# The first norm's modulation loaded and used by feature quarters, in a two-block transformer kernel on one core

## The chip, the cores and the metric

The kernel runs on one core of one Trainium2 chip. The metric is the device time of one execution in microseconds, the median of three runs. A core has five engines that each work through their own list of instructions in order: TensorE (PE, whose weight loads the profile lists apart as PEld), VectorE (DVE), ScalarE (ACT), GpSimd (POOL) and SyncE (SP), which issues the transfers here. An engine that stands before an instruction whose input is missing waits there, and what is behind it in its list waits too.

## The reference

Two blocks run one after the other on 256 tokens and 256 context tokens of width 1024. The first block has two layers; only the start of layer 0 is touched by the change:

```python
mod = silu(c) @ w_ada[li] + b_ada[li]               # 6 * 1024 values; the same for the context with c_ctx
sh1, sc1, g1, sh2, sc2, g2 = split(mod, 6)
m  = unpack(modulate(rms_norm(x,  norm1_w), sh1,  sc1)  @ w_in[li])
mc = unpack(modulate(rms_norm(xc, norm1_w), sh1c, sc1c) @ w_in[li])
...                                                  # attention, a gated recurrence, a Fourier mix
x = x + g1 * merge(...)
x = x + g2 * conv_ffn(modulate(rms_norm(x, norm2_w), sh2, sc2), ...)

def rms_norm(x, w):    return x * rsqrt(mean(x * x) + 1e-6) * w
def modulate(h, shift, scale): return h * (1 + scale) + shift
```

So before the first product with `w_in` can start, the kernel needs the token sums of squares, their roots, and the shift and scale of the features that the product reads. Shift and scale together are 2048 columns of `w_ada`, 8 MB of the 252 MB that the kernel reads.

## The kernel before

Activations lie with features on the 128 partitions: `x` is a tile of 8 feature steps (k) by 512 tokens (v = 0 the 256 tokens, v = 1 the context). Weights arrive as plain float32 tiles `raw`; ACT rounds them to `wH` (line 137) and DVE takes the rest `wL` (line 139). Each product of a feature step is three matmuls on TensorE, `wH` with the high part of the activation, `wH` with its low part, `wL` with the high part (line 151). The activation's parts are the tiles `hm`, a pair for each k.

The stages of the start, with the names that the text uses:

- **Squares.** `sq_add` squares `x` on ACT in pieces of 256 tokens and adds them up on DVE into `acc`; `rstd` lets TensorE add up over the partitions (line 204), ACT takes the root (line 210), DVE inverts and puts it on a diagonal (`dg`), TensorE spreads it over the partitions (line 222).
- **Modulation.** `ada_half` loads half of shift and half of scale, 16 tiles of 256 KB, and multiplies them with `csil`, the silu of the conditions, into one PSUM tile `pa` (line 315). `ada_out` copies that to `araw` on ACT, turns it on TensorE (line 373) and adds the bias on DVE into `mod`; `ada_scale` makes the factor `A`.
- **Norm and modulate.** `norm` multiplies `x` by the spread root on DVE (line 394). `modulate` then makes the high part `hm` on ACT (line 406), the full value `y` on POOL (line 408, two buffers) and the low part on DVE (line 409).
- **First products.** `rec(0)` makes four outputs, two forget gates from one weight (PSUM tiles `pg`) and query and gate from another (`ps`). They are 4 outputs x 8 feature steps x 3 = 96 products, each on 512 tokens. Both weights come in two parts of four feature steps, `wpart(*w, 0, 4)` and `(4, 8)`.
- After that `values()` follows, and beside it `ada_steps`, which loads the other columns of `w_ada` into `araw` tiles (line 332) and multiplies them (line 335). `ada_out` and `ada_steps` share the three buffers of `araw`.

`pa` has one buffer, so the product of the next piece of modulation waits until DVE has read the piece before:

```python
return self.ps.tile([P, 512], F32, name=tag, tag=tag, bufs=2 if tag in ("pg", "ps") else 1)
```

The order of the instructions on each engine is set when the program is built: a scheduler simulates the program and lists each engine's work by readiness and priority (`urgent` raises it). On the chip that order is fixed. All transfers here go through SP's list, in order.

Of the kernel before, what the change touches and what calls it, by code (L numbers as in the profile page):

```python
# [18 lines left out]
P = 128  # L19
EPS = 1e-6  # L20
KD = 8
# [34 lines left out]
class Builder:  # L56
# [104 lines left out]
    def gemm(self, W, c0, acts, T, t0=0, pt=None, tag=None):  # L161
# [10 lines left out]
        self.tick()  # L172
        return pt

    def gemm_nat(self, W, acts, t0, pt, p0):

        nc = self.nc
        H, L = W
        n, tot = 0, 3 * len(acts)
        for k, (h, l) in enumerate(acts):  # L180
            for c, a in ((h, H), (h, L), (l, H)):
                self.product(pt[:, p0:p0 + 256], c[:, t0:t0 + P], a[:, k, :], n == 0, n == tot - 1)
                n += 1
        self.tick()
# [46 lines left out]
    def setup(self, es):  # L231
# [21 lines left out]

        self.x = self.cp.tile([P, 8, 512], F32, name="x")
        self.mods = []

    def late_setup(self):
        nc, d = self.nc, self.d
# [4 lines left out]
        for a, b in ((0, 4), (4, 7)):  # L263
# [3 lines left out]
        self.sub = self.cp.tile([P, 2, P], F32, name="sub")  # L267
        nc.sync.dma_start(self.sub, bass.AP(tensor=d["subln"].tensor, offset=d["subln"].offset,
                                            ap=[[0, P], [P, 2], [1, P]]))

        v = self.vec("lam").rearrange("p (l a b) -> p l a b", l=2, a=2)
        pr = self.sml("lpr", [P, 4], bufs=1)
# [4 lines left out]
        nc.scalar.activation(ex, pl[:, 0:4], AF.Exp)  # L277
        self.nlam = self.cp.tile([P, 2], F32, name="nlam")
        for li in range(2):
            init = 0.8 - 0.6 * math.exp(-0.3 * li)  # L280
            nc.vector.tensor_scalar(self.nlam[:, li:li + 1], ex[:, 2 * li + 1:2 * li + 2], ex[:, 2 * li:2 * li + 1],
                                    init, op0=OP.subtract, op1=OP.subtract)
            nc.vector.tensor_scalar(self.sub[:, li], self.sub[:, li], 1.0 - init, None, op0=OP.mult)

        lb = self.vec("lb").rearrange("p (l c) -> p l c", l=2)
        w = self.sml("lbw", [P, 4, 4], bufs=1)
# [8 lines left out]
        nc.vector.tensor_scalar(self.lb1[:, 1], self.lb1[:, 0], -1.0, 1.0, op0=OP.mult, op1=OP.add)  # L295


    def ada_half(self, li, b, tags):

        nc, d = self.nc, self.d  # L300
        if b == 0:
            self.mods.append(self.cp.tile([P, 2, 48], F32, name=f"mod{li}"))
        pa = self.psum("pa")
        for k in range(KD):
            src = d["w_ada"][li, k * P:(k + 1) * P, 0:2048].rearrange("p (m h c) -> p h m c", m=2, h=2)[:, b]
            if tags[2 * k]:
                raws = [self.ring(tags[2 * k + m], [P, 512]) for m in range(2)]
                for m in range(2):
                    nc.sync.dma_start(raws[m], src[:, m])
            else:  # L310
                raw = self.wp.tile([P, 2, 512], F32, name="raw", tag="raw", bufs=3)
                nc.sync.dma_start(raw, src)
                raws = [raw[:, 0], raw[:, 1]]
            for g in range(4):
                nc.tensor.matmul(pa[32 * g:32 * g + 32, 0:256], self.csil[:, k, :],
                                 raws[g // 2][:, (g % 2) * 256:(g % 2) * 256 + 256],
                                 start=k == 0, stop=k == KD - 1)
        self.ada_out(li, pa, [(g // 2) * 8 + b * 4 + (g % 2) * 2 for g in range(4)], 2)

    def ada_steps(self, li, b):  # L320

# [231 lines left out]
        return oT  # L553


    def layer(self, li, states):
        nc, d = self.nc, self.d
        T = 512 if li == 0 else 256
# [1 line left out]
        h = [self.pair("hm", 512, F32R) for _ in range(KD)]  # L560
        if li == 0:
            self.rush = False
            tags = ["e"] * 4 + ["mo"] * 4 + ["uf"] * 2 + ["va"] * 2 + ["ka"] * 2 + ["qa"] * 2
            self.ada_half(0, 0, tags)
            first = [(self.wtiles(), d["w_in"][0, i]) for i in (8, 6)]
            for w in first:
                self.wpart(*w, 0, 4)
            tags = ["Kp"] * 3 + ["Qp"] * 3 + ["Sd", "So"] + ["vh"] * 2 + ["fg"] * 2 + ["kk"] * 2
            self.ada_half(0, 1, [None] * 2 + tags)
            for w in first:  # L570
                self.wpart(*w, 4, 8)
        pb = [None] * 2
        for v in (1, 0):
            with self.urgent():
                pb[v] = self.rstd(states[v])[:, 0:256]
        tags = ["on", "on", "aT", "ks", "qh", "sg", "tot"]
        n = [(k, v, self.norm(pb[v], v, k, tags[(k + 1 - v) % 7])) for k in range(0, KD, 2) for v in (1, 0)]
        mod = self.mods[li]
        A1 = self.cp.tile([P, 2, 8], F32, name=f"A1{li}")
        for k0 in (0, 4):  # L580
            self.ada_scale(li, 1, A1, k0, k0 + 4)
            for k, v, t in n[k0:k0 + 4]:
                self.modulate(t, v, k, A1, mod[:, :, 0:8], h)
        if li == 0:
            self.late_setup()
        acts = h
        W = lambda i: self.wload(d["w_in"][li, i])
        mo = [None] * 8
        va, qa, kT = {}, {}, {}
# [36 lines left out]
                nc.scalar.copy(vn[s].rearrange("p a c -> p (a c)"), pt)  # L626

        def rec(j, tag=None):
            w = first[0][0] if li == j == 0 else W(8 + 2 * j)
            fg = [self.ring("fg", [P, 2, 256]) for _ in range(2)]  # L630
            kk = [self.ring("kk", [P, 2, 256]) for _ in range(2)]
            for a in range(2):
                pt = self.gemm(w, a * P, acts, 512)
# [8 lines left out]
            w = first[1][0] if li == j == 0 else W(6 + j)  # L642
            pt = self.gemm(w, 0, acts, T, tag=tag)
            q = self.ring("qh", [P, T])
            nc.scalar.copy(q, pt)
            pt = self.gemm(w, P, acts, T, tag=tag)
# [628 lines left out]
    def build(self):  # L1275
        nc, tc = self.nc, self.tc
        with ExitStack() as es:
# [11 lines left out]
            st = [dict(), dict()]  # L1289
            for k in range(0, KD, 2):  # L1290
                nc.sync.dma_start(self.x[:, k:k + 2], self.d["xin"][:, k:k + 2])
            for k in range(KD):
                for v in (1, 0):
# [99 lines left out]
def layout(inp):  # L1393
# [5 lines left out]
    o["w_ada"] = g["w_ada"]  # L1399
    win = []  # L1400
    for li in range(2):
        w = g["w_in"][li].reshape(1024, 24, P)
# [57 lines left out]
```

## Time and profile before

| | |
|---|---|
| median of three runs | 1746.14 us (1745.81 to 1746.52) |
| the profiled execution | 1746.53 us, its span 1744.7 us |
| TensorE busy | 1694.4 us, 97% of the span |
| DVE, ACT, POOL busy | 1020.3, 844.6, 314.8 us |
| read from memory | 252.42 MB, 145 GB/s over the span |
| TensorE's mean granted clock | 0.99 |

The span is what the profiler saw; about 1.8 us lie around it. Times of rows are microseconds from the span's start.

### The profile page before, as it was taken

The page shows a single profiled execution, that of the slowest core. Times are in us where ns is not written, and L with a number is a line of the kernel's source. Part 1 is how long each engine was busy: PE and PEld are TensorE (multiplying, and loading weights), DVE is VectorE, ACT ScalarE, POOL GpSimd, SP SyncE. Part 2 cuts the span into 40 slices and gives each one's busy share as a digit, 9 for nine tenths or more (in the row PEclk, how much of TensorE's full clock was granted, in tenths as well). Part 3 has the DMA queues.
Part 4 walks back from the last instruction along what each step waited for, and adds up shares of the span by engine and source line. Part 5 has one row for each costly group of instructions (what it writes and reads, how often), then busy time and mean ns, then how long its engine had stood idle before and what let it go on. Part 6 is the DMA issues. An engine that isn't in the chain of part 4 may idle for free.

```text
span 1744.7 us, 29180 instructions
## 1 busy us (share of the span) xinstructions
PE 1694.4 (97%) x11598; PEld 1445.1 (83%) x11598; DVE 1020.3 (58%) x1835; ACT 844.6 (48%) x1472; POOL 314.8 (18%) x406
## 2 busy tenths in 40 slices
PE   6999899999999999989999899999999999999998
PEld 2766676887777788868788899999999999998988
DVE  4445756565433454455766776767666655655557
ACT  4435645453321343243755554665444565556554
POOL 1322210130100011234140210122202203212200
PEclk9999999999999999989999899999999999999999
DMA  9664111334445322335423446555555555444442
GB/s 331 231 199 151 46 44 36 98 119 147 161 140 187 130 97 72 103 112 176 147 91 105 153 149 207 176 176 190 178 189 180 178 175 173 156 146 148 155 135 71
DMA packets 86705, 255.45 MB, mean 146 GB/s; under 512 B 8823, under 2 KB 20471, under 8 KB 86568
## 3 DMA queue, kind: packets, MB, share of 16 engines
q1 hardware_dynamic: 86568, 253.58, 43.9%
q8 instruction: 91, 1.49, 0.3%
q14 instruction: 46, 0.38, 0.1%
HBM read 252.42 MB, written 1.13 MB: 145 GB/s over the span
## 4 chain that ended last, share of the span: by engine, by line
PE 92%; DVE 3%; ACT 2%; DMA 2%; issue 1%; POOL 0%; SPq 0%; ACTq 0%; DVEq 0%; POOLq 0%
PE pg L151 46%; PE ps L151 16%; PE ph L151 8%; PE pu L151 8%; PE pa L335 3%; PE ph L485 2%; PE ps L1198 1%; PE ps L740 1%; PE pa L1235 1%; PE ph L1221 1%; PE pu L778 1%; PE pu L1134 1%; ACT wH L137 1%; DMA x<-in_xin_dram 0%; DVE wL L139 0%
## 5 line engine op out<-in xcount | busy, mean ns | idle before, releaser
L139 DVE TENSOR_TENSOR wL<-raw,wH 128x1024 fp32r<-128x1024 f32 (+2 forms) x388 | 444.8, 1177 | 251.3 <-ACT wH L137 243.4
L137 ACT CAST wH<-raw 128x1024 fp32r<-128x1024 f32 (+2 forms) x388 | 370.6, 994 | 397.8 <-PE pg L151 206.1
L151 PE MATMUL pg<-hx,wH 128*128 128x256 f32 x1184 | 220.1, 283 | 0.7 <-ACT vv L1175 0.7
L151 PE MATMUL pg<-hm,wH 128*128 128x512 f32 (+1 forms) x736 | 204.2, 361 | 6.0 <-DVE x L699 3.5
L151 PEld LDWEIGHTS pg<-hx,wH 128*128 128x128 f32 x1184 | 183.6, 189 | 5.0 <-issue 3.6
L151 PE MATMUL pg<-hx,wL 128*128 128x256 f32 x592 | 168.4, 284 | 0.0
L151 PEld LDWEIGHTS pg<-hm,wH 128*128 128x128 f32 x736 | 127.2, 189 | 49.4 <-issue 13.5
L151 PE MATMUL pg<-hm,wL 128*128 128x512 f32 (+1 forms) x368 | 130.7, 355 | 0.0
L887 POOL TENSOR_TENSOR tt<-tt 128x512 f32<-128x512 f32 (+1 forms) x44 | 44.6, 1015 | 441.5 <-DVE tt L884 441.5
L151 PE MATMUL pg<-h,wH 128*128 128x256 f32 (+1 forms) x464 | 115.9, 338 | 1.7 <-ACT h L406 1.4
L151 PE MATMUL ps<-h,wH 128*128 128x256 f32 (+1 forms) x464 | 114.1, 335 | 0.0
L151 PEld LDWEIGHTS pg<-hx,wL 128*128 128x128 f32 x592 | 111.1, 188 | 1.7 <-issue 0.9
L151 PEld LDWEIGHTS pg<-h,wH 128*128 128x128 f32 x464 | 80.2, 193 | 16.9 <-ACT wH L137 5.9
L151 PEld LDWEIGHTS ps<-h,wH 128*128 128x128 f32 x464 | 80.3, 192 | 9.4
L151 PE MATMUL pg<-hid,wH 128*128 128x256 f32 (+1 forms) x360 | 81.8, 318 | 1.1 <-ACT wH L137 1.1
L151 PEld LDWEIGHTS pg<-hm,wL 128*128 128x128 f32 x368 | 69.5, 189 | 12.1 <-issue 2.6
L151 PE MATMUL ps<-hid,wH 128*128 128x256 f32 (+1 forms) x344 | 78.0, 319 | 0.0
L151 PE MATMUL pg<-h,wL 128*128 128x256 f32 (+1 forms) x232 | 77.9, 336 | 0.0
L151 PE MATMUL ps<-h,wL 128*128 128x256 f32 (+1 forms) x232 | 77.8, 335 | 0.0
L151 PE MATMUL pg<-wH,hx 128*128 128x256 f32 x384 | 74.8, 285 | 0.0
L151 PE MATMUL pg<-wH,hm 128*128 128x256 f32 x384 | 72.9, 285 | 0.0
L199 POOL TENSOR_TENSOR acc<-acc,y 128x256 f32<-128x256 f32 x40 | 37.6, 948 | 193.5 <-ACT y L198 192.7
(414 smaller groups left out, 3794.8 us busy)
## 6 DMA issues: line engine op xcount, KB each, us to landing
raw<-in_w_up_dram SPq DMA_DIRECT2D x88, 512.0 KB, 4.7
araw<-in_w_ada_dram SPq DMA_DIRECT2D x80, 512.0 KB, 4.5
raw<-in_attn_w_in_dram SPq DMA_DIRECT2D x80, 512.0 KB, 4.4
raw<-in_conv_w_in_dram SPq DMA_DIRECT2D x64, 512.0 KB, 4.5
raw<-in_w_in_dram SPq DMA_DIRECT2D x48, 512.0 KB, 5.3
raw<-in_w_down_dram SPq DMA_DIRECT2D x32, 384.0 KB, 3.7
raw<-in_w_down_dram SPq DMA_DIRECT2D x32, 320.0 KB, 3.0
raw<-in_conv_w_out_dram SPq DMA_DIRECT2D x16, 512.0 KB, 4.6
```

Source lines behind the costliest of these rows:

```text
L137: nc.scalar.copy(H[:, a:b], raw)
L139: nc.vector.tensor_tensor(L[:, a:b], raw, H[:, a:b].bitcast(F32), OP.subtract)
L151: self.mm = self.nc.tensor.matmul(pt, a, b, start=start, stop=stop)
L199: st["last"] = i, (nc.vector if last else nc.gpsimd).tensor_tensor(st["acc"], st["acc"], sq, OP.add)
L335: nc.tensor.matmul(pa[32 * g:32 * g + 32, :], self.csil[:, k, :], raw[g // 2][:, g % 2], start=k == 0, stop=k == KD - 1)
L485: nc.tensor.matmul(pt[:, v, c:c + P], l, m, start=True, stop=True)
L740: nc.tensor.matmul(pts[i][:, :n], qa[h][rr, qt * P:(qt + 1) * P], kT[h][rr, k0 * P:k0 * P + n], start=True, stop=True)
L778: nc.tensor.matmul(po[:, 0:P], aT[:, b * P:(b + 1) * P], va[kb // 2][:, kb % 2, hh * P:(hh + 1) * P], start=b == 0, stop=b == nk - 1)
L887: nc.gpsimd.tensor_tensor(tt[1], tt[0], tt[1], OP.mult)
L1134: nc.tensor.matmul(pc[32 * n:32 * n + 32, 0:256], hsel, sq[n // 2][:, n % 2], start=True, stop=True)
L1198: nc.tensor.matmul(ps[v][:, o:o + ks.stop - ks.start], qh[g][rr[v], i, qs], kh[g][rr[v], i, ks], start=True, stop=True)
L1221: nc.tensor.transpose(pt[:, v, k * P:(k + 1) * P], u["e"][v][:, k * P:(k + 1) * P], self.ident)
```

## The change

Three things change in the start of layer 0; the mathematics stays.

1. `ada_half` becomes `ada_quarter`: shift and scale come in four pieces of 256 features (two feature steps), 8 tiles of 256 KB each. The columns of `w_ada` are regrouped on the host. After each quarter the modulation, the factor `A` and the two feature steps of `hm` are made. The products of a quarter are 128 columns wide, where those of a half were 256.
2. The four outputs of `rec(0)` are made together, feature step by feature step (`gemms`).
3. TensorE adds up the squares: ACT and DVE take turns in squaring 512 tokens of a feature step, and 32 matmuls of one column add them up (line 586 of the changed kernel). The root is taken for each 128 tokens (line 592). A table load for the root is put at the end of `setup`, and the small setup of the gates moves ahead of it.

```diff
+    def gemms(self, groups, acts):
+        last = len(acts) - 1
+        for k, (h, l) in enumerate(acts):
+            for (H, L), c0, t0, pt in groups:
+                ts = slice(t0, t0 + pt.shape[-1])
+                for n, (a, c) in enumerate(((H, h), (H, l), (L, h))):
+                    self.product(pt, a[:, k, c0:c0 + P], c[:, ts], k == 0 and n == 0, k == last and n == 2)
...
+        self.gates_setup()
+
+        tc.keep_in_program_order(nc.scalar.preload_act_table_set("sqrt_and_others"))
...
-    def ada_half(self, li, b, tags):
+    def ada_quarter(self, b, tags):
...
+            raw = self.ring(tags[k], [P, 512])
+            nc.sync.dma_start(raw, d["w_ada"][0, k * P:(k + 1) * P, 512 * b:512 * b + 512])
             for g in range(4):
-                nc.tensor.matmul(pa[32 * g:32 * g + 32, 0:256], self.csil[:, k, :],
-                                 raws[g // 2][:, (g % 2) * 256:(g % 2) * 256 + 256],
+                nc.tensor.matmul(pa[32 * g:32 * g + 32, 0:P], self.csil[:, k, :], raw[:, g * P:(g + 1) * P],
                                  start=k == 0, stop=k == KD - 1)
-        self.ada_out(li, pa, [(g // 2) * 8 + b * 4 + (g % 2) * 2 for g in range(4)], 2)
+        self.ada_out(0, pa, [(g // 2) * 8 + b * 2 + g % 2 for g in range(4)], 1)
...
+    def start(self, h):
...
+        for k in range(KD):
+            sq = self.ring(tags[k % 7], [P, 512])
+            if k % 2:
+                nc.vector.tensor_tensor(sq, x[:, k], x[:, k], OP.mult)
+            else:
+                nc.scalar.activation(sq, x[:, k], AF.Square)
+            for t in range(4):
+                nc.tensor.matmul(pn[t][:, 0:1], sq[:, t * P:(t + 1) * P], self.ones[:, 0:1],
+                                 start=k == 0, stop=k == KD - 1)
+        with self.urgent():
+            for v in (1, 0):
+                rs = self.sml("rs", [P, 2])
+                for j in range(2):
+                    nc.scalar.activation(rs[:, j:j + 1], pn[2 * v + j][:, 0:1], AF.Sqrt, bias=self.eps,
+                                         scale=1.0 / 1024)
+                nc.vector.reciprocal(rs, rs)
+                dg = self.ring("Kh", [P, 2, P])
+                for j in range(2):
+                    t = 2 * v + j
+                    nc.vector.tensor_scalar(dg[:, j], self.ident, rs[:, j:j + 1], None, op0=OP.mult)
+                    nc.tensor.matmul(pb[:, t * P:(t + 1) * P], self.ones, dg[:, j], start=True, stop=True)
+        n = {}
+        for b, rt in enumerate((["e"] * 4 + ["mo"] * 4, ["uf"] * 2 + ["va"] * 2 + ["ka"] * 2 + ["qa"] * 2,
+                                ["Kp"] * 4 + ["Qp"] * 4, ["Sd", "So"] + ["vh"] * 2 + ["fg"] * 2 + ["kk"] * 2)):
+            self.ada_quarter(b, rt)
+            if b < 2:
+                for w in first:
+                    self.wpart(*w, 4 * b, 4 * b + 4)
+            k = 2 * b
+            self.ada_scale(0, 1, A1, k, k + 2)
+            for v in (1, 0):
+                t = self.norm(pb[:, v * 256:v * 256 + 256], v, k, tags[(2 * b + 1 - v) % 7])
+                self.modulate(t, v, k, A1, self.mods[0][:, :, 0:8], h)
...
-            for k in range(KD):
-                for v in (1, 0):
-                    self.sq_add(st[v], self.x[:, k, v * 256:(v + 1) * 256], last=True)
-            st = self.layer(0, st)
+            st = self.layer(0, None)
```

The built programs show where the scheduler put this. On ACT, from the gates' setup to the first `hm`, the kernel before has (`lex` and `lbw` belong to the gates, `sd` is the root):

```order
L290 ACTIVATE lbw<-lbw 128x8
L277 ACTIVATE lex<-pu 128x4
L195 ACTIVATE acc<-x 128x256 x2
L198 ACTIVATE y<-x 128x256 x14
L210 ACT_TABLE_LOAD
L210 ACTIVATE sd<-pg,eps 128x2 x2
L370 COPY araw<-pa 128x256
L137 CAST wH<-raw 128x1024 x2
L406 ACTIVATE hm<-on,mod_162,A_371 128x256 x4
```

The changed kernel has on ACT, from the same place (`rs` is the root now):

```order
L268 ACT_TABLE_LOAD
L299 ACT_TABLE_LOAD
L299 ACTIVATE lex<-pu 128x4
L584 ACTIVATE on<-x 128x512
...
L137 CAST wH<-raw 128x1024 x2
L592 ACT_TABLE_LOAD
L592 ACTIVATE rs<-pu,eps 128x1
L592 ACTIVATE rs<-ps,eps 128x1 x2
L592 ACTIVATE rs<-ph,eps 128x1
L383 COPY araw<-pa 128x128
L137 CAST wH<-raw 128x1024
L419 ACTIVATE hm<-on,mod_211,A_136 128x256 x4
```

The two casts of the first weights stand ahead of the roots now; the exponential's table is loaded again behind the root's, and the root's once more behind the casts.

On DVE, from the second diagonal to the first low parts of `hm`, the changed kernel has (rows `<-x,ph` are the norm, `mod` and `A` the modulation of the first quarter):

```order
L598 TENSOR_SCALAR Kh<-ca,rs 128x128 x2
L407 TENSOR_TENSOR on<-x,ph 128x512 x2
L407 TENSOR_TENSOR aT<-x,ph 128x512
L407 TENSOR_TENSOR ks<-x,ph 128x512
L407 TENSOR_TENSOR qh<-x,ph 128x512
L407 TENSOR_TENSOR sg<-x,ph 128x512
L407 TENSOR_TENSOR tot<-x,ph 128x512
L388 TENSOR_TENSOR mod_211<-pa,vt 128x2 x4
L139 TENSOR_TENSOR wL<-raw,wH 128x1024
L400 SCALAR_TENSOR_TENSOR A_136<-mod_211,vt 128x2 x2
L422 TENSOR_TENSOR hm<-y,hm 128x256 x2
```

Seven norms of all four quarters stand in one piece ahead of the first quarter's modulation, and wait for the roots of both halves of the tokens; before, seven norms stood ahead of the first half's modulation as well, four of them behind the first root alone.

On TensorE the changed kernel has, from the last tiles of the first quarter (`e`, `mo`) to the third quarter (`Kp`, `Qp`):

```order
L329 MATMUL pa<-mo,csil 32x128 x5
L599 MATMUL ph<-Kh,ca 128x128 x2
L329 MATMUL pa<-mo,csil 32x128 x11
L599 MATMUL ph<-Kh,ca 128x128 x2
L386 MATMUL pa<-ca,araw 128x128
L329 MATMUL pa<-uf,csil 32x128 x8
L329 MATMUL pa<-va,csil 32x128 x8
L329 MATMUL pa<-ka,csil 32x128 x8
L329 MATMUL pa<-qa,csil 32x128 x8
L151 MATMUL pg<-hm,wH 128x512 x2
L151 MATMUL ps<-hm,wH 128x512 x2
...
L329 MATMUL pa<-Kp,csil 32x128 x16
```

The modulation's products stand in whole quarters between pairs of feature steps, where before they stood in single tiles between the products; and the first quarter's products stand behind the spread of the first root.

## Rows read from the trace of the kernel before

**Rows 1.** Windows: start:end, length, busy PE, PEld, DVE, ACT, POOL, granted clock, DMA share, GB/s.

```profile
0.00:66.00 66.00, 47.66 (x264) 25.53 (x266) 28.31 (x79) 28.52 (x57) 13.19 (x23) 0.97 0.78 276
66.00:150.00 84.00, 84.00 (x549) 58.43 (x546) 41.28 (x90) 35.19 (x74) 22.82 (x36) 1.00 0.65 219
150.00:250.00 100.00, 95.30 (x615) 70.14 (x614) 63.65 (x151) 57.92 (x131) 21.32 (x36) 0.98 0.20 63
...
52.00:56.00 4.00, 4.00 (x16) 1.78 (x13) 2.13 (x5) 2.06 (x3) 3.29 (x5) 0.70 0.89 311
```

**Rows 2.** Timeline, PEld: second and fourteenth tile of modulation, and the sums over partitions.

```profile
14.66 0.19 PEld L315 LDWEIGHTS pa<-e,csil 128*32 128x32 f32 x4 [0.39 <-DMA e<-in_w_ada_dram]
16.97 0.52 PEld L204 LDWEIGHTS pg<-ca,acc 128*128 128x128 f32 x4 [0.76 <-DVE acc L199]
22.74 0.14 PEld L315 LDWEIGHTS pa<-ka,csil 128*32 128x32 f32 x4 [0.53 <-DMA ka<-in_w_ada_dram]
```

**Rows 3.** Timeline, ACT: start, length, line, what [idle before it and releaser].

```profile
2.39 1.28 ACT L252 ACT_TABLE_LOAD   x1 [2.39 <-DMA cin<-in_cin_dram]
3.69 0.22 ACT L252 ACTIVATE csil<-cin 128x16 f32<-128x16 f32 x1
8.84 0.72 ACT L195 ACTIVATE acc<-x 128x256 f32<-128x256 f32 x2 [3.24 <-DMA x<-in_xin_dram]
17.62 0.26 ACT L210 ACTIVATE sd<-pg,eps 128x2 f32<-128x2 f32 x1 [0.57 <-PE pg L204]
25.64 2.05 ACT L137 CAST wH<-raw 128x1024 fp32r<-128x1024 f32 x2
28.20 2.08 ACT L406 ACTIVATE hm<-on,mod,A 128x256 fp32r<-128x256 f32 x4 [0.52 <-DVE A L387]
```

**Rows 4.** Timeline, spread of the root on PE, and DVE's norms, modulation, low parts, masks.

```profile
18.59 0.49 PE L222 MATMUL pg<-dg,ca 128*128 128x128 f32 x2
19.84 0.69 DVE L394 TENSOR_TENSOR on<-x,pg 128x512 f32<-128x512 f32 x1
21.64 0.68 DVE L394 TENSOR_TENSOR tot<-x,pg 128x512 f32<-128x512 f32 x1
26.60 0.37 DVE L375 TENSOR_TENSOR mod<-pa,vt 128x4 f32<-128x4 f32 x4
31.25 0.76 DVE L409 TENSOR_TENSOR hm<-y,hm 128x256 fp32r<-128x256 f32 x2
40.07 0.90 DVE L266 CAST msk<-e 128x512 uint8<-128x512 f32 x2 [3.99 <-DMA e<-in_msk_dram]
```

**Rows 5.** Timeline, the first product on PE, and the second half's modulation on three engines.

```profile
29.35 0.50 PE L151 MATMUL pg<-hm,wH 128*128 128x512 f32 x1
47.71 0.38 PE L373 MATMUL pa<-ca,araw 128*128 128x128 f32 x2
48.73 0.60 ACT L406 ACTIVATE hm<-sg,mod,A 128x256 fp32r<-128x256 f32 x1 [3.63 <-DVE A L387]
51.30 0.43 DVE L409 TENSOR_TENSOR hm<-y,hm 128x256 fp32r<-128x256 f32 x1 [0.46 <-POOL y L408]
```

**Rows 6.** The chain that ended last, in order of time: start, length, engine, tile, line.

```profile
36.44 1.00 PE pa L315 x16
37.44 0.43 PE pg L151
37.87 0.56 PE pa L315 x4
44.14 3.73 PE ps L151 x16
64.76 1.84 PE pa L335 x12
79.20 0.99 PE pa L335 x8
```

**Rows 7.** Page, transfers by line: count, size, median time to landing.

```profile
araw<-in_w_ada_dram SPq DMA_DIRECT2D x80, 512.0 KB, 4.5
```

More of the change, by code (lines that the diff above doesn't have):

```diff
@@ L269, in late_setup, with lam0, gates_setup @@
                                             ap=[[0, P], [P, 2], [1, P]]))
+        for li in range(2):
+            nc.vector.tensor_scalar(self.sub[:, li], self.sub[:, li], 1.0 - self.lam0(li), None, op0=OP.mult)
+    def lam0(self, li):
+        return 0.8 - 0.6 * math.exp(-0.3 * li)
+    def gates_setup(self):
+        nc = self.nc
         v = self.vec("lam").rearrange("p (l a b) -> p l a b", l=2, a=2)
@@ L295, in late_setup @@
         nc.vector.tensor_scalar(self.lb1[:, 1], self.lb1[:, 0], -1.0, 1.0, op0=OP.mult, op1=OP.add)
-    def ada_half(self, li, b, tags):
+    def ada_quarter(self, b, tags):
         nc, d = self.nc, self.d
         if b == 0:
-            self.mods.append(self.cp.tile([P, 2, 48], F32, name=f"mod{li}"))
+            self.mods.append(self.cp.tile([P, 2, 48], F32, name="mod0"))
         pa = self.psum("pa")
         for k in range(KD):
[L305 to L313, printed above, removed]
+            raw = self.ring(tags[k], [P, 512])
+            nc.sync.dma_start(raw, d["w_ada"][0, k * P:(k + 1) * P, 512 * b:512 * b + 512])
             for g in range(4):
-                nc.tensor.matmul(pa[32 * g:32 * g + 32, 0:256], self.csil[:, k, :],
-                                 raws[g // 2][:, (g % 2) * 256:(g % 2) * 256 + 256],
+                nc.tensor.matmul(pa[32 * g:32 * g + 32, 0:P], self.csil[:, k, :], raw[:, g * P:(g + 1) * P],
                                  start=k == 0, stop=k == KD - 1)
-        self.ada_out(li, pa, [(g // 2) * 8 + b * 4 + (g % 2) * 2 for g in range(4)], 2)
+        self.ada_out(0, pa, [(g // 2) * 8 + b * 2 + g % 2 for g in range(4)], 1)
     def ada_steps(self, li, b):
@@ L553, in hgrn @@
         return oT
+    def start(self, h):
+        nc, d, x = self.nc, self.d, self.x
+        A1 = self.cp.tile([P, 2, 8], F32, name="A10")
+        first = [(self.wtiles(), d["w_in"][0, i]) for i in (8, 6)]
+        tags = ["on", "on", "aT", "ks", "qh", "sg", "tot"]
+        ph = self.psum2()
+        pn, pb = [self.psum("ps"), ph[:, 0], self.psum("pu"), self.psum("ps")], ph[:, 1]
+        for k in range(KD):
[31 more added lines that the diff above has]
+                self.modulate(t, v, k, A1, self.mods[0][:, :, 0:8], h)
+        return first
     def layer(self, li, states):
@@ L562, in layer @@
             self.rush = False
[L563 to L572, printed above, removed]
-        for v in (1, 0):
[L574 to L584, printed above, removed]
-            self.late_setup()
-        acts = h
+            first = self.start(h)
+            self.late_setup()
+        else:
+            pb = [None] * 2
+            for v in (1, 0):
+                with self.urgent():
+                    pb[v] = self.rstd(states[v])[:, 0:256]
+            tags = ["on", "on", "aT", "ks", "qh", "sg", "tot"]
+            n = [(k, v, self.norm(pb[v], v, k, tags[(k + 1 - v) % 7])) for k in range(0, KD, 2) for v in (1, 0)]
+            mod = self.mods[li]
+            A1 = self.cp.tile([P, 2, 8], F32, name=f"A1{li}")
+            for k0 in (0, 4):
+                self.ada_scale(li, 1, A1, k0, k0 + 4)
+                for k, v, t in n[k0:k0 + 4]:
+                    self.modulate(t, v, k, A1, mod[:, :, 0:8], h)
+        acts, mod = h, self.mods[li]
         W = lambda i: self.wload(d["w_in"][li, i])
@@ L628, in rec @@
         def rec(j, tag=None):
-            w = first[0][0] if li == j == 0 else W(8 + 2 * j)
+            pts = [None] * 4
+            if li == j == 0:
+                pts = [self.pg() for _ in range(2)] + [self.psum(tag)[:, :T] for _ in range(2)]
+                self.gemms([(first[i // 2][0], i % 2 * P, 0, pts[i]) for i in range(4)], acts)
+            else:
+                w = W(8 + 2 * j)
             fg = [self.ring("fg", [P, 2, 256]) for _ in range(2)]
@@ L641, in rec @@
                         nc.vector.tensor_scalar(kk[s][:, a], kk[s][:, a], om, None, op0=OP.mult)
-            w = first[1][0] if li == j == 0 else W(6 + j)
-            pt = self.gemm(w, 0, acts, T, tag=tag)
+            if pts[2] is None:
+                w = W(6 + j)
+            pt = self.gemm(w, 0, acts, T, tag=tag) if pts[2] is None else pts[2]
             q = self.ring("qh", [P, T])
             nc.scalar.copy(q, pt)
-            pt = self.gemm(w, P, acts, T, tag=tag)
+            pt = self.gemm(w, P, acts, T, tag=tag) if pts[3] is None else pts[3]
             sg = self.ring("sg", [P, T])
@@ L1398, in layout @@
     o["cin"] = np.stack([g["c"][0], g["c_ctx"]], axis=-1).reshape(8, P, 2).transpose(1, 0, 2)
-    o["w_ada"] = g["w_ada"]
+    wa = g["w_ada"].copy()
+    wa[0, :, 0:2048] = wa[0, :, 0:2048].reshape(1024, 2, 4, 256).transpose(0, 2, 1, 3).reshape(1024, 2048)
+    o["w_ada"] = wa
     win = []
```

7 lines of the change are left out of this document (2 added, 5 removed).

## Prediction

> **What bounds the kernel now.** I read the page first: TensorE is busy 97% of the span, so a change in the start can win only what TensorE idles there, or must do less. Windows by stage say how much that is: 18.3 us of the first 66 us are idle (66.00 less 47.66), none of the next 84 [rows 1]. What the start gains or loses is therefore carried on: no gap behind it swallows a delay.
>
> Then I read the start engine by engine. Tiles of `w_ada` pace it: from the second tile's first use (14.66) to the fourteenth's (22.74) twelve tiles of 256 KB came in 8.08 us, 0.673 each [rows 2]. The root, taken at 17.62, is early [rows 3]; four norms follow at 0.60 us apiece, the difference of 19.84 and 21.64 in three steps [rows 4]. The first quarter of the norm is thus waiting when the modulation comes (26.60), the first `hm` is at 28.20 and the first product at 29.35 [rows 3 to 5]. From there TensorE alternates between products and modulation. The chain shows what that costs: 16 products in 3.73 us, 0.233 each; 16 modulation instructions (two k of a half) in 1.00, but four alone 0.56 where 0.25 would be their share, and one product alone 0.43. A return trip costs 0.31 + 0.20, about 0.5 us. The 96 products end at 64.76, where the last run of L335 begins [rows 6].
>
> **The change part by part.** I place each new piece by the order of the changed lists and by durations from rows.
>
> *Transfers.* Tile n of 256 KB lands at 14.66 + 0.673(n - 2), a weight part counting as two. The first quarter (8 tiles) is there at 18.7, the first weights' parts at 20.0 and 21.4, the second quarter at 26.8, the third at 33.5, the last at 40.2. The bytes are the same.
>
> *Squares.* 32 matmuls of one column are 64 instructions; four took 0.52 [rows 2], so 8.3 us, from about 9.5 (first squares at 8.84 [rows 3]) to 17.8. That is hidden: the roots wait for something later. If they did not, it would be as early as the old sums.
>
> *Root.* The preload does not help. Behind it stands the gates' exponential, which loads its own table again, and then the root's is loaded a second time. The two early loads (2 x 1.28) fit into ACT's idle 3.24 us ahead of the squares [rows 3]; without that cover they would cost up to 2.6. The last load stands behind two casts that wait for weights. The second lands at 21.4, a cast takes 1.05 (2.05 for two), the load 1.28: 23.7. The second half of the tokens comes first; its pair is the first and third root, at most 0.26 each, so the third starts at 24.2. From the old root's start to the end of its spread were 1.46 us (17.62 to 18.59 + 0.49) [rows 3, 4]: 25.7. TensorE stood waiting for that with 11 of the first quarter's matmuls behind it: 2.75 k at 0.25 and a return trip, 1.2, then the other spread 0.49: 27.4.
>
> Does a table switch cost more than its load? ACT's first load ends at 2.39 + 1.28 = 3.67 and the activation behind it starts at 3.69 [rows 3], so I take 1.28. [...]
>
> *Norms.* All seven wait for both spreads and stand ahead of the modulation: 27.4 + 7 x 0.60 = 31.6. From the modulation's start to the first `hm` were 1.60 us (26.60 to 28.20), with the same weight rest in between: 33.2, and the first product 1.15 later at 34.4, against 29.35: **5.0 us later**. Behind the waiting product nothing can run; the second quarter's matmuls (there since 26.8) wait too, for the one buffer of `pa`, until 32.0.
>
> *Products by quarter.* Width 128 has no row. Two k of width 256 take 1.00, one k of width 512 (x8, L335) 0.99 [rows 6]: halving the width halved the time. So a quarter is between 2.0 (half of a half's 4.0) and 4.0 (no saving); I take 2.0, the trend of the two rows. Then TensorE runs:
> - four products 34.4 to 35.3, then a wait for the low parts. The third low part ended 3.8 after the first `hm` (28.20 to 32.01) [rows 3, 4]: 37.0. Eight more to 38.9; second feature step with the turning of the second quarter (a return trip) to 42.2.
> - The second quarter's `A` stands behind a mask cast on DVE. Its transfer is tile 42, 41.6 by the pace; in the kernel before tile 38 was due at 38.9 and cast at 40.07 [rows 4], so 42.8. Cast 0.45, `A` and handover 0.2: first `hm` 43.45. Meanwhile the third quarter's matmuls, to 44.5; four products from 44.6; ACT makes four `hm` (2.08) and then copies (0.4), so the turning ends at 46.4; low parts 3.0 after `hm` (48.73 to 51.73 [rows 5]): 46.45. Twenty more products: 51.1.
> - last quarter 2.3, to 53.4; 24 products and a turning, 6.1, to 59.5. The turning, at 58.3, puts the first `hm` 1.0 later (47.71 to 48.73) at 59.3. Four L335 matmuls (0.99 and a trip) to 61.0; four products to 61.9; then two L335 whose tile needs the `araw` buffer that this turning frees: 58.5 + 4.5 [rows 7] = 63.0. With them 63.7, and 20 products: **68.4**.
>
> *Four outputs at once* costs and saves no product. It makes all four end together, so the next weights are cast later; six L335 matmuls cover that as before (1.84 [rows 6]). Four reads of PSUM at up to 0.52 (a quarter of 2.08), a cast and a rest of 1.2 from 1.4 ahead of the end take 2.9, so up to 1.1 is left uncovered. I take 0, since the kernel before runs the same reads and casts behind its last product under the same cover; the 1.1 goes into the upper bound.
>
> *Sum.* Products end 68.4 - 64.76 = 3.6 later, with two more L335 done by then (0.5): **+3.1**. Against the profiled execution (1746.53) that is 1749.6; against the median, 0.4 lower, **1749.2**. From both sides: kind ends (mask at 41.6, `araw` 1 us faster, roots at 0.17) leave +1.2; quarters of 4.0 us on the path (the last two) and half of the uncovered cast give +7.6.
>
> **Rivals.**
> 1. *The start runs at the pace of the transfers*, as the quarters would allow: root by 20, norms done by 24, first product about 24 (the second cast and rest end at 23.7), end about 24 + 22.4 (96 products) + 9 (quarters, trips, L335) = 56, 8 us earlier: 1738. For it: the data are there. Against it: the casts and the seven norms stand ahead in fixed lists. The point from which it wins 0.2% is a first `hm` 6.6 us ahead of mine, at 26.6.
> [...]
> 3. *The scheduler's other order pays or costs further on.* TensorE idles 4.7 of the 100 us from 150 to 250 [rows 1], in attention, and the order there differs. All of it won: 1744.5; as much lost: 1754.
> 4. *No effect*, the lists notwithstanding: that needs 1 and the losses to cancel; it lies in the range of the others.
>
> **How the numbers follow.** Forecast 0.50, its own range 1747.3 to 1753.7; clock 0.13; order pays 0.15, order costs 0.08; pace of the transfers 0.14. A measurement tells 0.2% (3.5 us) from no change. Of the forecast 0.30 lies below +3.5 and 0.20 above; with the order that pays, same is 0.45; slower is 0.20 + 0.13 + 0.08 = 0.41; faster is the first rival, 0.14. The range leaves out most of that rival and the far end of the third: 1742.5 to 1754.0.
>
> **What would show it.** Right: ACT's roots behind the second cast, near 24; norms in one run near 27 to 31.6; first product near 34; TensorE idle some 5 us ahead of the first spread; mask cast ahead of the second `A`; products ended near 68. Wrong: the first `A` before 29, a quarter's 32 matmuls far from 2.0 us, `values` starting before 67, or a difference that opens only behind 150 us.

## The result, and the profile after

The changed kernel takes 1762.84 us, median of 4 runs (1762.12 to 1763.35), against 1746.33 for the kernel before in the same comparison: ratio 1.0086, 95% interval 1.0074 to 1.0097, so 13 to 17 us slower. The forecast was 1749.2 in a range to 1754.0. The profiled execution has a span of 1761.3 us.

Windows of the changed kernel, columns as in [rows 1]; the first three are stretches shown there:

```profile
0.00:66.00 66.00, 52.31 (x436) 42.91 (x437) 24.89 (x78) 25.09 (x41) 11.67 (x23) 0.95 0.80 280
66.00:150.00 84.00, 81.75 (x538) 57.47 (x538) 39.97 (x81) 35.30 (x73) 22.28 (x34) 1.00 0.64 210
150.00:250.00 100.00, 90.28 (x580) 67.72 (x577) 60.97 (x146) 58.42 (x134) 23.07 (x36) 0.91 0.18 60
185.00:237.00 52.00, 43.03 (x299) 34.86 (x297) 30.57 (x68) 31.42 (x69) 14.55 (x21) 0.84 0.12 39
34.00:38.00 4.00, 4.00 (x59) 3.43 (x51) 2.48 (x8) 2.34 (x5) 2.70 (x4) 0.52 1.00 355
```

TensorE idles 9.7 us of 150 to 250, where it idled 4.7 [rows 1], and its granted clock is 0.91 there in place of 0.98. That is far behind the start, in code that the diff does not touch.

The start itself, timeline of TensorE (first and last sum, first quarter, the two spreads L599, turning, second quarter, first product):

```profile
8.97 0.58 PE L586 MATMUL ps<-ca,on 128*128 128x1 f32 x2 [3.51 <-ACT on L584]
...
22.22 0.56 PE L586 MATMUL ps<-ca,on 128*128 128x1 f32 x2
22.71 1.93 PE L329 MATMUL pa<-e,csil 128*32 128x128 f32 x32
...
25.41 1.22 PE L599 MATMUL ph<-Kh,ca 128*128 128x128 f32 x4
...
27.81 0.71 PE L599 MATMUL ph<-Kh,ca 128*128 128x128 f32 x4
28.36 0.27 PE L386 MATMUL pa<-ca,araw 128*128 128x128 f32 x1
33.21 1.08 PE L329 MATMUL pa<-uf,csil 128*32 128x128 f32 x16 [4.57 <-issue]
...
36.78 1.19 PE L151 MATMUL pg<-hm,wH 128*128 128x512 f32 x2
```

and of ScalarE (the Exp load over the early one of root, the casts, root's load again, first modulation) and VectorE (norms, modulation):

```profile
5.62 1.28 ACT L268 ACT_TABLE_LOAD   x1
6.91 1.28 ACT L299 ACT_TABLE_LOAD   x1
8.20 0.17 ACT L299 ACTIVATE lex<-pu 128x4 f32<-128x4 f32 x1
...
21.42 1.05 ACT L137 CAST wH<-raw 128x1024 fp32r<-128x1024 f32 x1 [0.60 <-DMA raw<-in_w_in_dram]
22.48 1.28 ACT L592 ACT_TABLE_LOAD   x1
23.78 0.26 ACT L592 ACTIVATE rs<-pu,eps 128x1 f32<-128x1 f32 x1
...
34.34 2.08 ACT L419 ACTIVATE hm<-on,mod,A 128x256 fp32r<-128x256 f32 x4 [4.49 <-DVE A L400]
```

```profile
28.56 1.28 DVE L407 TENSOR_TENSOR on<-x,ph 128x512 f32<-128x512 f32 x2 [0.92 <-PE ph L599]
...
32.16 0.68 DVE L407 TENSOR_TENSOR tot<-x,ph 128x512 f32<-128x512 f32 x1
32.75 0.35 DVE L388 TENSOR_TENSOR mod<-pa,vt 128x2 f32<-128x2 f32 x4
```

The order of events is the forecast one: the root at 23.8 behind two casts is on time, the norms in one run to 32.8 and the first `hm` at 34.3 are about 1 us late (it was 28.20 before [rows 3]), the first product at 36.8 is 2.4 late. The chain that ended last shows the third quarter's matmuls (1.88 us), the end of the first products, 67.69 (64.76 before [rows 6]; forecast 68.4), and a wait for a transfer into `araw` on either side:

```profile
43.21 1.88 PE pa L329 x64
...
58.03 3.70 DMA araw<-in_w_ada_dram
...
67.69 1.02 PE pa L348 x8
68.72 3.94 DMA araw<-in_w_ada_dram
```

Where the rest opens is seen by following the same instruction through two traces. For every TensorE instruction that a kernel shares with before: its start, less its start in before; medians by stretch of before's time, in us. Columns: the changed kernel, and five of the kernels of the experiments below.

```
before's time  changed  start after,  order before  order before  squares before,  squares before,
                        order before  from 185      185 to 260    order held       order free
 60-70           3.2       1.9           3.8           4.1           -4.4             -3.5
100-120          5.1       1.9           4.6           5.1           -4.4             -2.2
180-190          2.1       1.9           1.7           2.1           -4.4             -5.1
210-220         11.0       1.8           3.3           4.1           -4.3              0.7
260-280         12.0       1.8           3.8           4.3           -4.2              1.0
400-450         14.8       2.0           3.9           3.4           -4.2              3.0
900-1000        14.4       0.4           2.6           4.6           -5.6              5.5
1400-1500       16.6       0.3           2.4           5.5           -6.2              5.5
```

At 60 to 70 us the change costs 3.2 in this trace, near the forecast's 3.1. It is +2.1 at 180 to 190, +11.0 at 210 to 220, and +16.6 in the end. (A single execution places the whole by some 2 us: a kernel below whose start is before's own stood 2.0 late from 60 us on.)

### The profile page after: what moved, and what is told of

The parts are those of the page before. It is cut to its first block, busy times and chain, and to the rows that moved or that the text cites. A ratio compares the mean times of both kernels' runs of the same rounds, so it can differ in the third digit from the quotient of the medians.

```text
span 1761.3 us, 29537 instructions
## 1 busy us (share of the span) xinstructions
PE 1703.2 (97%) x11782; PEld 1469.5 (83%) x11782; DVE 1018.5 (58%) x1837; ACT 846.6 (48%) x1467; POOL 315.8 (18%) x406
## 4 chain that ended last, share of the span: by engine, by line
PE 91%; ACT 3%; DVE 3%; DMA 2%; issue 1%; ACTq 0%; DVEq 0%; SPq 0%
PE pg L151 45%; PE ps L151 16%; PE pu L151 8%; PE ph L151 7%; PE pa L348 3%; PE ph L498 2%; PE ps L1254 1%; PE pa L1291 1%; PE ps L796 1%; DMA araw<-in_w_ada_dram 1%; PE ph L1277 1%; ACT wH L137 1%; PE pu L834 1%; PE pa L329 1%; DVE wL L139 1%
## 5 line engine op out<-in xcount | busy, mean ns | idle before, releaser
L151 PE MATMUL pg<-hx,wH 128*128 128x256 f32 x1168 | 216.8, 284 | 0.8 <-ACT vv L1231 0.7
L151 PE MATMUL pg<-hm,wH 128*128 128x512 f32 (+1 forms) x736 | 203.3, 361 | 4.3 <-DVE x L755 4.1
L151 PEld LDWEIGHTS pg<-hx,wH 128*128 128x128 f32 x1168 | 180.4, 188 | 5.3 <-issue 3.6
L151 PE MATMUL pg<-hx,wL 128*128 128x256 f32 x584 | 165.9, 284 | 0.0
L151 PEld LDWEIGHTS pg<-hm,wH 128*128 128x128 f32 x736 | 126.8, 189 | 43.5 <-issue 12.0
L151 PE MATMUL pg<-hm,wL 128*128 128x512 f32 (+1 forms) x368 | 131.0, 356 | 0.0
L151 PE MATMUL ps<-h,wH 128*128 128x256 f32 (+1 forms) x512 | 127.6, 339 | 0.0
L151 PE MATMUL pg<-h,wH 128*128 128x256 f32 (+1 forms) x512 | 125.2, 335 | 0.0
L151 PEld LDWEIGHTS pg<-hx,wL 128*128 128x128 f32 x584 | 110.0, 188 | 1.7 <-issue 0.9
L151 PEld LDWEIGHTS pg<-h,wH 128*128 128x128 f32 x512 | 87.0, 191 | 16.9 <-ACT wH L137 7.5
L151 PEld LDWEIGHTS ps<-h,wH 128*128 128x128 f32 x512 | 89.9, 196 | 11.1 <-DVE h L422 0.8
L151 PE MATMUL ps<-h,wL 128*128 128x256 f32 (+1 forms) x256 | 86.5, 338 | 0.0
L151 PE MATMUL pg<-h,wL 128*128 128x256 f32 (+1 forms) x256 | 85.2, 333 | 0.0
L151 PEld LDWEIGHTS pg<-hm,wL 128*128 128x128 f32 x368 | 69.2, 188 | 14.4 <-issue 4.9
L151 PE MATMUL pg<-wH,hx 128*128 128x256 f32 x384 | 74.8, 285 | 0.0
L151 PE MATMUL ps<-hid,wH 128*128 128x256 f32 (+1 forms) x338 | 74.0, 312 | 0.0
L151 PE MATMUL pg<-wH,hm 128*128 128x256 f32 x384 | 73.8, 289 | 0.0
L151 PE MATMUL pg<-hid,wH 128*128 128x256 f32 (+1 forms) x322 | 71.3, 314 | 0.0
```

What stands on the lines that cost most here:

```text
L151: self.mm = self.nc.tensor.matmul(pt, a, b, start=start, stop=stop)
```

## Experiments: is it the start or the order behind it?

Two theories. *Order*: the scheduler, given another start, lists the unchanged code behind it in another order, and that costs most. *Start*: late data cost all of it. The code behind the first four products is the same, instruction for instruction, so one kernel's order can be held in the other: an edge in issue order alone, without a wait, from each instruction to the next of its engine.

```
for r in order_of_the_other[engine]:
    i = traced[engine][-1 - r]
    if prev is not None:
        tc.add_manual_dep(i, prev.name, NoSync, reason="pin")
    prev = i
```

One thing else had to be made equal: the changed start takes four turns fewer of the counter that picks a PSUM bank, so the banks of the later feed-forward parts differ. `self.gi += 4` in the changed kernel, or `self.gi -= 4` in before, evens that out.

> The changed kernel's start (quarters, sums on TensorE, four products at once), but every engine's instructions behind it held in the order of the kernel before, with the same PSUM banks. Order theory (the start costs 3 to 5 us, the other 11 to 13 come from the order that the scheduler picked behind it): 1749 to 1752 us, with the delay against before at +3 to +5 from 60 us to the end. Start theory (the late data itself costs all of it): about 1762 us, with steps near 185 to 220 us again.

Measured: 1748.94 us, ratio to before 1.0004 (0.9995 to 1.0012).

> The start of before, with every engine's instructions behind it held in the order and the PSUM banks of the changed kernel. Order theory: 1757 to 1760 us, its +11 to +13 opening near 185 to 220, 300 to 400 and 1100 to 1200 us. Start theory: 1746 us, within 2.

Measured: 1769.32 us, ratio 1.0123 (1.0106 to 1.0141): slower than the changed kernel itself, and beyond the 1757 to 1760 that the order theory expected. The start theory falls on both: the new start with the old order costs 0.7 us (-0.9 to +2.1), the old start with the new order 21. Not all of the 21 is the loss looked for: measured as in the table, some 13 us are there at 100 to 120 us already, where the changed kernel is 5 late; the rest opens behind 185 us. The new order fits its own start better than the old one.

> The changed kernel with the rotation of PSUM banks of its feed-forward parts begun where before begins it (one counter; the changed start takes four turns fewer of it), the order left to the scheduler. Order theory: the step of some 2 us near 1100 to 1200 us is gone (1760 to 1761 us) and that of 185 to 220 us stays. Start theory: 1762.8 us, within 1.

Measured: 1762.03 us, ratio 1.0081 (1.0067 to 1.0095): the banks are not what costs here.

> Before with only that rotation begun where the changed kernel begins it, the order left to the scheduler. Order theory: the scheduler's order behind 420 us differs and moves the time by 1 to 4 us, in either direction (1743 to 1750 us). Start theory: no start is changed, so 1746.3 us within 0.5.

Measured: 1754.82 us, ratio 1.0042 (1.0030 to 1.0055), beyond the 1 to 4 that I expected. Nothing changed in the source but a counter, and the time moved by 7 us. The lists of VectorE and ScalarE are before's up to about 260 us and differ behind that, so it may be the order again; the banks alone were not tried there.

Next, where. In the changed kernel with before's banks, before's order is held in one stretch alone (`order_of_the_other` cut by before's times).

> The changed start; the scheduler's own order up to 185 us, and from there on the order of before on every engine (banks as in before). If the loss lies in the order of the scan and attention stretch at 185 to 225 us itself: before + 2 to + 5 us (1748 to 1752). If it is the order ahead of it, at 66 to 185 us, that leaves the later chain uncovered: before + 10 or more (1757 and up). If all is late data: before + 16.

Measured: 1748.87 us, ratio 1.0011 (1.0000 to 1.0021). So the loss lies in the order from 185 us on.

> The changed start; the order of before (and its banks) is held from 185 to 260 us alone, ahead of it and behind it the scheduler orders. If the +8 between 185 and 225 us comes from the order of that stretch: it is gone, and before + 4 to + 8 is left (1752 to 1756: + 4 as with the order held from 185 us on, and what the free order behind 260 us costs, 0 to 4). If it comes from the state that the stretch is entered in: before + 12 or more.

Measured: 1751.67 us, ratio 1.0021 (1.0011 to 1.0031), a little less than the 1752 to 1756 expected. Holding 75 us of the order takes back 11 of the 15 us (1.0086 to 1.0021). Not all 11 arise there: left free behind 260 us, the scheduler now lists VectorE and ScalarE nearly as in before, not as in the changed kernel (of VectorE's instructions from 270 to 420 us, 99% stand in before's order, 64% in the changed kernel's). The table parts the two. Between the rows of 180-190 and 260-280 us the delay grows by 9.9 us in the changed kernel and by 2.2 here, so some 8 us are the stretch's own; from there to the end by 4.6 and 1.2, so some 3 lie behind it. What else differs between the three held runs (1.0004, 1.0011, 1.0021) is not told apart: their intervals overlap.

The windows say what the stretch loses. With the order held throughout (`start_after_order_before`), TensorE's busy time and clock are those of before again (95.30 and 0.98 [rows 1]):

```profile
150.00:250.00 100.00, 95.28 (x604) 69.39 (x602) 63.91 (x150) 58.36 (x132) 21.30 (x36) 0.98 0.22 68
185.00:226.40 41.40, 36.68 (x285) 29.36 (x285) 28.60 (x67) 27.92 (x65) 9.87 (x17) 0.96 0.15 48
```

Both 185 to 237 us in the changed kernel and 185 to 226.4 here end with the first product behind the scan (below). TensorE idles 9.0 us there in the one and 4.7 in the other, and is busy 43.0 and 36.7 us, at a granted clock of 0.84 and 0.96. So of the 10.6 us that the stretch takes longer, by these two traces, some 4 are waits and some 6 are about the same work done more slowly. An estimate from the granted clocks gives about as much: 0.16 x 52.0 = 8.3 us kept back in the one, 0.04 x 41.4 = 1.7 in the other.

What is worse about that order? There, the scan of the recurrence (L498, then masked copies L513 and products L458 on VectorE, level after level) runs beside large products (L151) that fill TensorE's waits. The changed kernel's TensorE timeline, from its last product to the next:

```profile
211.65 0.28 PE L151 MATMUL pg<-wH,hm 128*128 128x256 f32 x1
211.85 1.16 PE L498 MATMUL ph<-Qp,Kh 64*128 64x128 f32 x16
...
220.23 2.08 PE L498 MATMUL ph<-Qp,Kh 64*128 64x128 f32 x16 [5.26 <-DVE Sd L513]
...
224.66 1.22 PE L498 MATMUL ph<-Qp,Kp 64*128 64x128 f32 x8 [1.31 <-DVE Sd L513]
...
236.99 0.73 PE L151 MATMUL pg<-hm,wH 128*128 128x512 f32 x2
```

and the same place with before's order held:

```profile
208.69 0.28 PE L151 MATMUL pg<-wH,hm 128*128 128x256 f32 x1
...
211.04 1.16 PE L498 MATMUL ph<-Qp,Kh 64*128 64x128 f32 x16
213.43 0.66 PE L828 MATMUL pu<-ca,e 128*128 128x128 f32 x4 [1.23 <-DVE mx L802]
216.10 1.32 PE L835 MATMUL pu<-va,aT 128*128 128x128 f32 x8 [2.01 <-ACT aT L830]
217.35 1.23 PE L498 MATMUL ph<-Qp,Kp 64*128 64x128 f32 x8
...
226.41 0.73 PE L151 MATMUL pg<-hm,wH 128*128 128x512 f32 x2
```

TensorE goes without a product to fill in for 25 us in the one (211.9 to 237.0) and for 17 in the other (209.0 to 226.4). In the changed kernel the products are used up while three levels of the scan are still to come, in before's order two. On VectorE, the masked copy for which TensorE waits 5.26 us stands behind two low parts of weights (`wL`) that no product reads before 237:

```profile
215.69 1.22 DVE L139 TENSOR_TENSOR wL<-raw,wH 128x1024 fp32r<-128x1024 f32 x1
216.83 0.35 DVE L468 TENSOR_TENSOR tot<-tot 128x192 f32<-128x192 f32 x1
217.10 0.68 DVE L800 TENSOR_REDUCE mx<-ps 128x1 f32<-128x512 f32 x1
217.70 1.75 DVE L139 TENSOR_TENSOR wL<-raw,wH 128x1024 fp32r<-128x1024 f32 x1
219.37 0.71 DVE L513 COPY_PREDICATED Sd<-msk,ph 128x512 f32<-128x512 uint8 x1
```

Do single displaced instructions like these carry the loss? Four runs hold the changed kernel's own order on every engine and move only what is named:

```
VectorE:  ... wL, tot, mx, wL, Sd ...       ->  ... tot, mx, Sd, wL, wL ...
ScalarE:  sigmoid, Exp, araw, root, Exp     ->  sigmoid, root, Exp, araw, Exp
```

> The changed kernel with its own order held on every engine: the control. Both theories: before + 15 (1761 to 1764), as the changed kernel.

Measured: 1763.42 us, ratio 1.0081 (1.0068 to 1.0094).

> The control, but on VectorE the two low-part casts that ran at 215.7 and 217.7 us stand behind the masked copy into Sd of 219.4 us; nothing else moves. If these two casts make the 5.3 us wait of TensorE: the copy at about 216.5, TensorE's wait 2.5 to 3 us shorter, the time 2 to 3 us below the control (before + 12 to + 13). If many small displacements add up and none counts alone: within 0.7 us of the control.

Measured: 1761.30 us, ratio 1.0071 (1.0059 to 1.0083), 2 us below the control with intervals that overlap. TensorE's waits for `Sd` from 180 to 232 us (us in total, times, longest), control first, say why it is not more:

```profile
PE ph L498 <- DVE Sd L513: 6.6, 2, 5.3
```

```profile
PE ph L498 <- DVE Sd L513: 5.6, 2, 3.2
```

The first wait falls from 5.3 to 2.5 us and the next, for the same tile one level on, grows from 1.3 to 3.2: 1.0 us of waiting is gained.

> The control, but on ScalarE the root into Sd (191.1 us) stands ahead of the first of the two exponentials (188.5 us), as in before; nothing else moves. If the root between them is what costs: one table load of 1.28 us less, TensorE's waits of 0.43 and 1.32 us for e shrink, 1 to 2 us below the control. If not: within 0.7 us.

Measured: 1764.37 us, ratio 1.0088 (1.0073 to 1.0104): no gain, though a table load of 1.28 us is saved. TensorE's list has the scores (L796) ahead of the scan there; with the exponential later they wait 2.4 us in one piece (0.4 and 1.3 in the control), and the same instructions behind them run some 3 us later than in the control.

> The control with both of these moves. If the two places are independent and each counts: 3 to 5 us below the control (before + 10 to + 12). If there are many small ones: within 1 us of the control.

Measured: 1763.13 us, ratio 1.0079 (1.0067 to 1.0091): unclear against the control. So neither place carries more than some 2 of the 15 us. Other places were not tried. What is shown is that the order costs the time, and that holding this stretch takes back 11 us, some 8 of them in it; that the cause is one level more of the scan in the open, at a granted clock of 0.84 in place of 0.96, is argued from the timelines and windows.

## Experiments: what the start's parts are worth

With before's order held, each part can be priced without the scheduler's answer to it. All start from `start_after_order_before` (1.0004), and one of them then lets the order go. The first takes the sums off TensorE:

```
-  for t in range(4):
-      nc.tensor.matmul(pn[t][:, 0:1], sq[:, t * P:(t + 1) * P], self.ones[:, 0:1], ...)
+  for v in (1, 0):
+      self.sq_add(st[v], x[:, k, v * 256:(v + 1) * 256], last=True)
```

> As start_after_order_before (before + 0.7, bounds -0.9 to + 2.1), but the squares are added on ScalarE and VectorE as before, with four instead of 64 small sums on TensorE; quarters, four products at once and the order of before stay. If the sums are hidden, as the prediction had it: the same within 1 us. If they hold back the first quarter's matmuls (in the changed kernel these begin at 22.6 us, 0.4 us behind the last sum): 2 to 4 us faster than start_after_order_before.

Measured: 1742.86 us, ratio 0.9969 (0.9957 to 0.9981): 6 us faster than with the sums on TensorE, and faster than before: more than either expectation. The sums were not hidden. Timeline of this kernel, TensorE, ScalarE and VectorE (norms, modulation):

```profile
12.74 2.60 PE L329 MATMUL pa<-e,csil 128*32 128x128 f32 x32 [7.38 <-ACT y L208]
...
14.91 1.28 ACT L587 ACT_TABLE_LOAD   x1
...
19.00 1.04 ACT L137 CAST wH<-raw 128x1024 fp32r<-128x1024 f32 x1 [0.89 <-DMA raw<-in_w_in_dram]
...
22.52 1.27 DVE L407 TENSOR_TENSOR on<-x,ph 128x512 f32<-128x512 f32 x2
...
26.70 0.35 DVE L388 TENSOR_TENSOR mod<-pa,vt 128x2 f32<-128x2 f32 x4
...
27.28 1.09 ACT L419 ACTIVATE hm<-on,mod,A 128x256 fp32r<-128x256 f32 x2 [5.77 <-DVE A L400]
...
60.07 1.06 PE L348 MATMUL pa<-araw,csil 128*32 128x512 f32 x8
```

Two things moved. The first quarter's matmuls begin at 12.7, not at 22.7 behind the last sum; its first tiles are there by about then (in the changed kernel their transfers, issued from 4.0 us on, took 8.4). And the scheduler put the root's table load at 14.9, ahead of the casts instead of behind them. The traces say that the second counts: the first `hm` waits for the norms here (the modulation starts at 26.70 behind them) as in the changed kernel (32.75, though the first quarter was turned at 28.4), and the norms start at 22.5 in place of 28.6. Sums that end at 22.8 would hold the roots until then wherever they stood; the load behind the casts adds 1 us (first root at 23.8). The two were not priced apart. First products end at 60.1 in place of 67.7.

> The start of squares_before_order_held (before - 5.4 with the order of before held), but the scheduler orders all that is behind it. If the order behind the start is the larger part: 8 to 16 us above the held one, before + 3 to + 11, though no instruction and no datum of its start differs. If order matters only through late data: before - 5.4 within 2.

Measured: 1752.57 us, ratio 1.0033 (1.0022 to 1.0044): the scheduler's own order takes 11 us from the same start, and turns 5 us of gain into 6 of loss.

> As start_after_order_before, but the first four outputs are accumulated one after the other again. If four at once is worth nothing (the prediction's sum had no gain or loss for it): the same within 1.5 us. If it is what lets the quarters pay: three outputs of 24 products at 0.233 us are then left behind the last quarter at 52 us in place of 24 products, 8 to 12 us slower (1757 to 1761).

```
-  self.gemms([(first[i // 2][0], i % 2 * P, 0, pts[i]) for i in range(4)], acts)
+  pt = self.gemm(w, a * P, acts, 512)        # and so for each of the four
```

Measured: 1749.10 us, ratio 1.0006 (0.9997 to 1.0015). The same, and its trace shows why: with the outputs written one after the other, the scheduler still alternates them, in the last quarter six products of one output and then six of the next. Writing them together only writes down what it does anyway; four outputs truly in sequence were not priced.

> As start_after_order_before, but the later quarters' norms stand on VectorE behind the first quarter's modulation, not ahead of it. If the six norms of 0.60 us ahead of the modulation are on the path (VectorE 27.9 to 32.1 us): first modulated tile at about 30 instead of 33.7 us, and 2.5 to 4 us faster than start_after_order_before (1745 to 1746.5). If the start is bound by something else (transfers into araw): within 1 us of it.

```
+  with self.tc.issue_after(m.ins) if b else ExitStack():     # m: first modulation's last low part
       t = self.norm(...)
```

Measured: 1747.87 us, ratio 0.9999 (0.9990 to 1.0007): at most 1 us or so, less than expected and not told from none (1.0004, 0.9995 to 1.0012). The first `hm` came at 30.38 in place of 33.68, but the second quarter's only at 40.23 in place of 41.96: its modulation (39.65 on VectorE) stands behind the low part of a weight whose transfer ScalarE awaited until 37.42, and TensorE, busy from 38 to 44 us without the hold, idles 2.1 us of it.

> squares_before_order_held with the later quarters' norms behind the first modulation as in norms_held. If the four norms (0.60 us each, 23.7 to 26.7 us) ahead of the first modulation are on the path: first modulated tile at about 24.5 in place of 27.3 us and before - 6.5 to - 8.5 (1739 to 1741). If the transfers or the araw buffers bound it: before - 5.4 within 1.

Measured: 1740.86 us, ratio 0.9962 (0.9949 to 0.9975), with the next one the fastest of all. First `hm` at 24.64, 2.6 us earlier than without the hold, of which about 1 reaches the end, if any (the intervals overlap).

> best_squares_before_norms_held without the early load of the root's table. As the prediction had it, the load is overwritten by that of Exp and root's is loaded again behind the squares, but in ScalarE's idle time ahead of the squares: the same within 1 us. If it held the squares back: up to 2.6 us faster (two loads of 1.28).

Measured: 1740.51 us, ratio 0.9963 (0.9951 to 0.9975): the early load costs nothing and brings nothing.

## Why the prediction was wrong

- **The step that failed** is the price of the order behind the start. The forecast's sum has no term for it, and rival 3 bounds it: "All of it won: 1744.5; as much lost: 1754." That took the 4.7 us that TensorE idled in before's attention as the most that another order can cost there. Idle time says what can be won by filling it. It does not bound what can be lost: the stretch from 185 us to the first product behind the scan takes 10.6 us longer than with before's order, with TensorE idle for 9.0 us in place of 4.7, at a granted clock of 0.84 in place of 0.96. Measured, the order costs 14 us (1.0086 against 1.0004); holding 185 to 260 us alone takes back 11, some 8 of them in that stretch. The rival named the place and the way, at a chance of 0.08 and a third of the size, and the prediction's own sign of being wrong, a difference that opens only behind 150 us, came. "What the start gains or loses is therefore carried on" holds with the order held (from 60 to 70 us to 400 to 450, +1.9 becomes +2.0, and -4.4 becomes -4.2), but a free order adds its own: 2.1 us at 185 became 11.
- **The start's sum**, +3.1, met 3.2 at 60 to 70 us in the changed kernel's trace, but with the order held the time says 0.7 (-0.9 to +2.1), so it was too high. That it came this near was in part luck: the terms were off both ways (the first product 2.4 us later than forecast, the products' end 0.7 earlier):
  - *Squares*, "hidden", 8.3 us to 17.8: they took 13.8, to 22.8, at 0.21 us an instruction where four of the old sums gave 0.13 [rows 2]. And they were not hidden: without them, and with the root where the scheduler then put it, the kernel is 6 us faster. I asked what the roots wait for in the given list (the load, right by 1 us), but not what the list would be without the sums.
  - *Root*: table load 22.5 to 23.8, forecast 22.4 to 23.7: right. The two spreads ended at 26.6 and 28.5, forecast 25.7 and 27.4; the fourth root waited 2.3 us for the first spread (it started at 26.67), which the forecast did not have. Behind a load the first activation starts 0.02 and 0.01 us on (22.48 + 1.28, then 23.78; 6.91 + 1.28, then 8.20), as it did in [rows 3], so taking 1.28 for a load was right.
  - *Preload*, useless and hidden: right (0.9962 with it and 0.9963 without, in the fastest kernel).
  - *Norms ahead of the modulation*: right in the trace (28.6 to 32.8, forecast 27.4 to 31.6); but holding them back brings at most 1 us at the end, so a late first `hm` is not carried on in full.
  - *Mask cast ahead of the second `A`*, first `hm` 43.45: 43.11. *`araw`*: the wait came as forecast and ended at 61.8, forecast 63.0.
  - *A quarter's matmuls*: the third's took 1.88 us at a granted 1.00, forecast 2.0; the second's took 3.6 (33.21 to 36.78) with 0.52 granted from 34 us on.
  - *Four at once*: 0, right, for a reason that I had not given.
- **Clock.** The forecast's chance of 0.13 for it was my estimate, and no run shows that term; what the traces showed in its place is a granted 0.52 from 34 to 38 us, where the second quarter's matmuls took 1.7 us longer than the third's at 1.00. TensorE had waited from 28.6 to 33.2 just ahead of them; that the wait lowered the clock is not shown, nor how much of the 1.7 us reached the end. The granted clock was low again behind 185 us (0.84 to 237 us), which cost more: by the estimate above 8.3 us were kept back there.
- **Pace of the transfers** (rival 1, 1738): the mechanism exists. Without the sums the products end at 60.1 and the time is 1742.9 with the order held. Its point of 26.6 for the first `hm` was passed only with the norms held too (24.6), at 1740.9. What kept it away was more than the casts and norms that I held against it: the norms are worth 2.6 us of the first `hm` (27.28 to 24.64), the sums and the root's place with them 6.4 (33.68, with the order held, to 27.28).

## What to carry to other kernels

Where a scheduler orders the code, a change in one place is two changes: its own, and another order behind it. Compare the lists behind the edit before pricing it, give the unknown order a range of both signs that idle time does not bound (here 7 us lost for a counter alone, 14 for this start, 11 for that without the sums), and separate the two by holding the old order. For instructions added to an engine that seems idle, ask also which list the scheduler would make without them, not only who waits for their result in the list at hand.

## What the runs showed of the hardware

A matmul of one column with a float32 tile as weights is two instructions (32 sums in the changed kernel's source, 64 instructions at its line 586); the 64 in an unbroken run took 0.21 us each (8.97 to 22.79), longer than the 0.13 that four alone had shown. Whether the clock is part of that is not shown: the trace's clock records begin at 27.6 us, but the first quarter's matmuls right behind the sums took 0.06 us each (32 in 1.93), like the second's at a granted 0.52, where the third's took 0.03. Two table loads in a row on ScalarE cost their 1.28 us each and 0.02 us besides (5.62 to 8.20). And from 185 us to the first product behind the scan TensorE idled 4.3 us more than with before's order, was granted 0.84 in place of 0.96, and was busy 6.3 us longer: the stretch lost more than the length of its waits.
